# Three ranks of priority for the recurrence stage of a two-block kernel: delta rule, gated branch, conditioning

## The chip, the cores and the metric

One Trainium2 chip, one core. The metric is the time of one execution on the device in microseconds, as the median of several executions. The profile is of one execution, and its times are those of the hardware profiler.

## What is computed

One sequence of 512 latent tokens with 256 context tokens, 1024 channels, everything in float32. `first_block` modulates a LayerNorm, projects it by `w_in` and sends the parts through three branches: a pooling branch, a delta rule and a gated recurrence, each of the last two in both directions. Their outputs, gated, go through `w_out`; a second block (a mixer, two feed-forward parts, latent attention) follows. What the change touches is these two recurrences, cut here to their steps:

```python
def step(S, inp):                       # delta rule, per head, 64 x 64 state
    w_t, k_t, v_t, kk_t, a_t = inp[:5]
    sa = jnp.einsum('bhvk,bhk->bhv', S, kk_t)
    S = (S * w_t[:, :, None, :] - sa[..., None] * (kk_t * a_t)[:, :, None, :]
         + v_t[..., None] * k_t[:, :, None, :])
    y = jnp.einsum('bhvk,bhk->bhv', S, inp[5]) if emit else None
...
def step(S, inp):                       # gated branch, per chunk of 32 tokens
    k_c, i_c, lf_c = inp[:3]
    g = jnp.cumsum(lf_c, axis=2)
    ...
    scores = jnp.einsum('bhtk,bhsk,bhtsk->bhts', q_c, k_c, rel)
    o = inter + jnp.einsum('bhts,bhsv->bhtv', scores, i_c)
    S = (jnp.exp(g_last[:, :, 0, :])[..., None] * S
         + jnp.einsum('bhsk,bhsv->bhkv', k_c * jnp.exp(g_last - g), i_c))
```

Conditioning is a product of the conditioning vectors with large weights (`mod_w`, `ada_w`), which gives shifts and scales; those of `ada_w` are needed only by the second block.

## The kernel before

Activations lie with channels on the partitions and tokens on the free axis. Every dense product (`dense`, L277) works in two float32r parts: the input is split into hh and hl, each weight block of 128 x 512 comes by DMA (`wblock`, L260) and is split by ScalarE (whi, L263) and VectorE (wlo, L264), and TensorE adds hh by whi, hl by whi and hh by wlo.

`block1` has three stages: LayerNorm and modulation into hh, hl; the recurrence stage; and the product with `w_out` with a LayerNorm. The recurrence stage consists of

- the **delta rule** (`rwkv_pair`), three pairs of heads p = 0 to 2 one after the other. A pair makes dense k, v and r, normalises kk (L631), and prepares (`rwkv_prep`): up-products for decay and a (L689), exponentials, and from them the operands BK and AR on VectorE (BK at L727). Then come three groups of four chunks. A group first makes scores of AR and BK (L763) and inverts a triangular matrix; a chunk updates the state (L926, L928, L934, L943), and the groups 1 and 2 give outputs (L959, L960). After each group but the last a gate (`gate`, a dense product and a sigmoid) is made. At the end of a pair is a readout (L658, L662).
- the **gated branch** (`hgrn_pair`), three pairs, each with a dense q, a dense i (transposed at L996), and for each direction a dense z and a unit (`hgrn_unit`), so six units, 0 to 5. A unit makes levels and gates on VectorE and ScalarE, then goes through its chunks: scores (L1084, L1087, L1091) copied by ScalarE into sct (L1099, L1102, L1104), outputs (L1111, L1112), state (L1120, L1125). A pair ends with a norm (L1008).
- **conditioning** (`ada`): half a block of `mod_w` and six blocks of `ada_w`, each block 16 transfers of 512 KB (L315) and the products of 4 columns of blocks with each (L318), then a copy (adaev) and transposes (L324).
- the **pooling branch** and, at the end, `gated`, the products of outputs and gates.

In PSUM, the delta rule has the banks mm, rsc and rch, the gated branch mf, conditioning ma. What follows in time on each engine is decided by the scheduler of the language when the program is built: it takes, of what is ready by its own estimate, the instruction with the lowest priority number, and that number counts up in the order in which the program is written. Before, a loop of six wrote one or two steps of the delta rule, one unit of the gated branch and one block of conditioning per turn, so the three had about the same priority at each point. On the chip each engine takes its instructions in the order so fixed.

Of the kernel before, what the change touches and what calls it, by code (L numbers as in the profile page):

```python
# [197 lines left out]
class B:  # L198
    def __init__(self, ctx, tc, d, taps=()):
        self.tc, self.nc, self.d, self.taps = tc, tc.nc, d, taps  # L200
        self.ctx = ctx
        self.cst = ctx.enter_context(tc.tile_pool(name="cst", bufs=1))
        self.wp = ctx.enter_context(tc.tile_pool(name="wp", bufs=3))
        self.hp = ctx.enter_context(tc.tile_pool(name="hp", bufs=1))
        self.streams = {"m": (self.wp, 2, 2)}
        self.load_consts()

    @contextmanager
    def banks(self, **spec):
# [217 lines left out]
    def block1(self):  # L427
        nc, tc, d = self.nc, self.tc, self.d
        mod = self.cst.tile([128, 24, 2], F32, name="mod")
        sc1 = self.cst.tile([128, 8, 2], F32, name="sc1")  # L430
        self.m2 = [self.cst.tile([128, 48, 2], F32, name=f"m2{l}") for l in range(2)]
        s = self.cond(self.cst)
# [15 lines left out]
        with ExitStack() as ctx:  # L448
            ctx.enter_context(self.banks(mm=2, rsc=2, rch=1, mf=2, ma=1))
            ctx.enter_context(self.stream("f", 2, 1))  # L450
            ctx.enter_context(self.stream("a", 3, 1))
            self.scr = ctx.enter_context(tc.tile_pool(name="scr", bufs=1, space=bass.MemoryType.DRAM))
            self.f1 = ctx.enter_context(tc.tile_pool(name="f1", bufs=1))
            self.f2 = ctx.enter_context(tc.tile_pool(name="f2", bufs=2))
            self.con1 = self.f1.tile([128, CONST.shape[1] - NCON], F32, name="con1")
            nc.sync.dma_start(self.con1, d["const"][:, NCON:])
            self.ymix = self.scr.tile([128, 8, NL], F32, name="ymix")
            self.ygate = self.scr.tile([128, 8, NL], F32, name="ygate")
            self.ar = [[self.f1.tile([128, 4, 2, 2 if g else 1, 64], F32, name=f"AR{g}{dd}") for dd in range(2)] for g in range(3)]
            self.tt = self.f1.tile([128, 8, 2, 64], F32, name="rtt")  # L460
            for a in (*chain(*self.ar), self.tt):
                nc.gpsimd.memset(a, 0.0)
            self.sct = [self.f1.tile([128, 2, 128], F32, name=f"sct{a}") for a in range(2)]
            for x in self.sct:
                nc.gpsimd.memset(x, 0.0)
            self.rwkv_lora()
            self.hgrn_lb()
            self.last = {}
            rw = chain.from_iterable(self.rwkv_pair(p) for p in range(3))
            hg = chain.from_iterable(self.hgrn_pair(p) for p in range(3))  # L470
            next(rw)
            for n in range(6):
                for _ in range(2 - n % 2):
                    next(rw, None)
                next(hg)
                if n == 0:
                    self.ada(s, 0, d["mod_w"], 1, 2, mod[:, 16:24], self.V("mod_b", 16, 8), "a")
                    self.pool_branch()
                l, g = divmod(n, 3)
                self.ada(s, 2, d["ada_w"][l], g, 4, self.m2[l][:, 16 * g:16 * g + 16],  # L480
                         self.V("ada_b_2", 48 * l + 16 * g, 16), "a")
            hh, hl = self.htiles()

            def gated(j, y=None):
                a = y or self.f1.tile([128, NL], F32, tag=("tw", "ta")[j % 2], name="ga")
                b = self.f1.tile([128, NL], F32, tag=("G", "km")[j % 2], name="gb")
                if y is None:
                    nc.sync.dma_start(a, self.ymix[:, j])
                nc.sync.dma_start(b, self.ygate[:, j])
                nc.gpsimd.tensor_tensor(b, a, b, op=ALU.mult)  # L490
                self.split(hh[:, j, 256:], hl[:, j, 256:], b)

            for j in (0, 1, 2, 3, 5, 6):
                gated(j)
            for _ in chain(rw, hg):
                pass
            for j in (4, 7):
                gated(j, self.last[j])
        self.xp = self.ctx.enter_context(tc.tile_pool(name="xp", bufs=1, reuse_waits="tile"))
# [115 lines left out]
    def rwkv_pair(self, p):  # L615
# [25 lines left out]
        for g in range(3):  # L641
            pre = self.rwkv_pre(g, bk, v)
            sts = []
            for i in range(4):
                sts.append(st)
                st = self.rwkv_chunk(g, i, ec[:, :, 4 * g + i], pre, st)
            if g:
                self.rwkv_out(g, sts, pre, y)
            if 3 * p + g < 8:
                self.gate(3 * p + g)  # L650
            if g < 2:
                yield

# [1127 lines left out]
```

## Time and profile before

| | us |
|---|---|
| median of 3 executions | 2722.59 |
| lowest and highest | 2719.27, 2726.03 |
| the profiled execution | 2736.78 |
| its span | 2735.0 |
| TensorE busy in the span | 2523.7 (92%) |
| VectorE, ScalarE busy | 1621.3 (59%), 1276.9 (47%) |
| mean granted clock of TensorE in the span | 0.947 |

A row of the view of waits gives the engine, the line that waited and its output, what it waited for, the total, how often and the longest. A row of the timeline gives start and duration, the instruction and, in brackets, the idle time before it and what ended that. The granted clock is a share of full speed: 1.00 is the upper of two levels, 0.50 the lower. The rows themselves stand in the section ahead of the prediction.

### The profile page before, as it was taken

The numbers are of one execution on the slowest core, as the hardware profiler recorded it, in microseconds if no ns is written. First come the engines' busy times: TensorE is split into PE (matmuls) and PEld (weight loads), VectorE is DVE, ScalarE is ACT, GpSimd is POOL, SyncE is SP. The second block draws the span as 40 slices with busy tenths as digits, with TensorE's granted clock in tenths as the row PEclk, the third lists the DMA queues.
The fourth block names the chain that finished last, engine by engine and source line by source line (L and its number), as shares of the span: only waits on it lengthen the run. The fifth ranks groups of instructions, "written<-read, shape, count | busy, mean of one in ns | idle before, by whom it ended". The sixth has DMA issues, their size and how long they took to land.

```text
span 2735.0 us, 53289 instructions
## 1 busy us (share of the span) xinstructions
PE 2523.7 (92%) x21320; PEld 1990.5 (73%) x21320; DVE 1621.3 (59%) x3815; ACT 1276.9 (47%) x2840; POOL 319.3 (12%) x432
## 2 busy tenths in 40 slices
PE   7989979979877989989899999999998999999998
PEld 3655646545546777777677888888886888888888
DVE  4566574576565656777856443344463767664665
ACT  3454454545455656556434332233344555542444
POOL 0121121122112000111110110011000000010010
PEclk9999989989887999999989999999998999999999
DMA  6233432434334211111231112212231102233325
GB/s 206 77 94 118 139 98 92 125 100 134 93 104 146 72 39 32 36 41 37 65 105 47 62 63 64 63 63 66 80 105 44 32 27 95 78 100 93 100 89 157
DMA packets 159016, 231.10 MB, mean 84 GB/s; under 512 B 12976, under 2 KB 90032, under 8 KB 158768
## 3 DMA queue, kind: packets, MB, share of 16 engines
q1 hardware_dynamic: 158768, 227.70, 26.7%
q8 instruction: 167, 2.74, 0.4%
q14 instruction: 81, 0.66, 0.1%
HBM read 217.95 MB, written 9.70 MB: 83 GB/s over the span
## 4 chain that ended last, share of the span: by engine, by line
PE 47%; DVE 2%; ACT 2%; issue 1%; POOL 1%; DMA 0%; POOLq 0%; SPq 0%; DVEq 0%; ACTq 0%
PE mm L277 39%; PE ms L1735 2%; PE mt L1754 1%; PE mv L351 1%; PE mt L1748 1%; PE mm L1685 1%; PE mf L277 0%; DVE hl L423 0%; DVE ht L421 0%; POOL qr L1669 0%; ACT hh L422 0%; DMA raw<-mla_w_out 0%; ACT whi L263 0%; ACT qrh L1705 0%; PE mm L1665 0%
## 5 line engine op out<-in xcount | busy, mean ns | idle before, releaser
L264 DVE TENSOR_TENSOR wlo<-raw,whi 128x512 fp32r<-128x512 f32 (+3 forms) x560 | 391.3, 701 | 395.1 <-ACT whi L263 236.6
L263 ACT CAST whi<-raw 128x512 fp32r<-128x512 f32 (+3 forms) x560 | 331.9, 594 | 462.8 <-PE mm L277 398.9
L277 PE MATMUL mm<-hh,whi 128*128 128x512 f32 (+1 forms) x1960 | 483.8, 360 | 28.0 <-ACT hh L422 13.6
L277 PE MATMUL mm<-hl,whi 128*128 128x512 f32 (+1 forms) x1960 | 457.3, 350 | 0.0
L277 PE MATMUL mm<-hh,wlo 128*128 128x512 f32 (+1 forms) x1960 | 455.3, 350 | 0.4 <-DVE wlo L264 0.4
L277 PEld LDWEIGHTS mm<-hh,whi 128*128 128x128 f32 x1960 | 332.4, 192 | 89.7 <-ACT hh L422 21.0
L277 PEld LDWEIGHTS mm<-hl,whi 128*128 128x128 f32 x1960 | 329.7, 193 | 46.8 <-issue 3.6
L277 PEld LDWEIGHTS mm<-hh,wlo 128*128 128x128 f32 x1960 | 328.9, 193 | 45.0 <-issue 2.0
L1233 POOL TENSOR_TENSOR fc<-fc,fc 128x768 f32<-128x768 f32 (+1 forms) x44 | 69.2, 1573 | 867.9 <-DVE fc L585 625.8
L277 PE MATMUL mm<-fh,whi 128*128 128x256 f32 (+1 forms) x616 | 136.3, 340 | 1.0 <-ACT fh L398 1.0
L583 DVE SCALAR_TENSOR_TENSOR fc<-mm,vec,fc 128x511 f32<-128x511 f32 (+1 forms) x132 | 86.8, 658 | 80.7 <-ACT fc L582 80.7
L277 PE MATMUL mm<-fl,whi 128*128 128x256 f32 (+1 forms) x616 | 130.5, 330 | 0.0
L277 PE MATMUL mm<-fh,wlo 128*128 128x256 f32 (+1 forms) x616 | 129.3, 328 | 0.0
L582 ACT ACTIVATE fc<-mm,vec 128x512 f32<-128x512 f32 (+1 forms) x132 | 81.4, 617 | 97.2 <-PE mm L277 97.2
L277 PEld LDWEIGHTS mm<-fh,whi 128*128 128x128 f32 x616 | 99.8, 190 | 15.8 <-issue 3.4
L318 PE MATMUL ma<-raw,cvs 128*32 128x256 f32 x832 | 95.6, 427 | 15.3 <-DMA raw<-ada_w 10.6
L277 PE MATMUL mf<-hh,whi 128*128 128x512 f32 (+1 forms) x360 | 103.6, 387 | 6.0 <-ACT whi L263 3.4
L277 PEld LDWEIGHTS mm<-fl,whi 128*128 128x128 f32 x616 | 99.0, 190 | 11.3 <-issue 0.5
L1197 DVE SCALAR_TENSOR_TENSOR xr<-mm,m,xr 128x512 f32<-128x512 f32 (+1 forms) x112 | 66.5, 597 | 67.0 <-PE mm L277 66.8
L277 PEld LDWEIGHTS mm<-fh,wlo 128*128 128x128 f32 x616 | 98.6, 190 | 10.4
L351 PE MATMUL mv<-sq,con 128*128 128x256 f32 (+1 forms) x240 | 84.3, 452 | 12.4 <-ACT sq L355 12.0
L277 PE MATMUL mf<-hl,whi 128*128 128x512 f32 (+1 forms) x360 | 95.4, 367 | 0.0
(545 smaller groups left out, 4383.6 us busy)
## 6 DMA issues: line engine op xcount, KB each, us to landing
raw<-ada_w SPq DMA_DIRECT2D x96, 512.0 KB, 4.6
raw<-ffn_up SPq DMA_DIRECT2D x176, 256.0 KB, 2.8
raw<-ffn_down SPq DMA_DIRECT2D x96, 256.0 KB, 2.7
raw<-w_in SPq DMA_DIRECT2D x66, 256.0 KB, 2.9
raw<-ab_w_in SPq DMA_DIRECT2D x50, 256.0 KB, 2.6
raw<-ffn_down SPq DMA_DIRECT2D x48, 192.0 KB, 2.4
raw<-mod_w SPq DMA_DIRECT2D x16, 512.0 KB, 7.6
raw<-w_out SPq DMA_DIRECT2D x32, 256.0 KB, 2.9
```

The costliest lines, as they stand in the source:

```text
L263: nc.scalar.copy(hi[:, :nk], raw[:, :nk])
L264: nc.vector.tensor_tensor(lo[:, :nk], raw[:, :nk], hi[:, :nk].bitcast(F32), op=ALU.subtract)
L277: nc.tensor.matmul(o, a[:, k], b[:, k0 + k, t:e], start=(k0 == 0 and j == 0 and k == 0), stop=(k0 + n == nk and j == 2 and k == n - 1))
L318: nc.tensor.matmul(acc[32 * b:32 * b + 32, c:c + 256], s[:, k, :], t[:, b], start=(k == 0), stop=(k == 7))
L351: self.nc.tensor.matmul(v[:, :x.shape[1]], self.C("ones"), x, start=(k == 0), stop=(k == 7))
L582: nc.scalar.activation(out[:, c0:c0 + cn], o[:, :cn], AF.Copy, scale=w[1])
L583: nc.vector.scalar_tensor_tensor(out[:, c0 + 1:c0 + cn], o[:, :cn - 1], w[0], out[:, c0 + 1:c0 + cn], op0=ALU.mult, op1=ALU.add)
L1197: nc.vector.scalar_tensor_tensor(x, o[:, :cn], gcol(m, 0 if c0 else 1), x, op0=ALU.mult, op1=ALU.add)
L1233: nc.gpsimd.tensor_tensor(g, g, u, op=ALU.mult)
L1685: nc.tensor.matmul(o[:, e], a[:, k, T], b[:, k], start=(i == 0), stop=(i == 5))
L1735: nc.tensor.matmul(o[:, at:at + cn], a, b, start=(j == 0), stop=(j == 4))
L1748: nc.tensor.transpose(tp[:, j], p[:, (c0 + j) * 128:(c0 + j + 1) * 128], self.C("ident"))
```

## The change

`ranks(3)` takes the current priority number as the base of rank 0 and sets rank 1 100000 above it and rank 2 200000 above it, and one more as the place after all of them. Inside `rank(i)` instructions are numbered on in that rank. The delta rule's steps are written in rank 0, the gated branch's units in rank 1, conditioning in rank 2. `behind(400)` moves the gates and the pooling branch back by 400 numbers in the delta rule's rank. The loop has nine turns instead of six, with a delta-rule step in each, a gated unit in six and a block of conditioning in seven; what is left of both recurrences is written after it, and `gated` after all ranks. No computation is changed, and the number of instructions is the same on every engine.

```diff
--- before.py
+++ after.py
@@ -204,6 +204,25 @@
         self.hp = ctx.enter_context(tc.tile_pool(name="hp", bufs=1))
         self.streams = {"m": (self.wp, 2, 2)}
         self.load_consts()
+
+    def ranks(self, n):
+
+        self.rank_at = [self.tc.cur_priority + 100000 * i for i in range(n + 1)]
+
+    @contextmanager
+    def rank(self, i):
+        tc, now = self.tc, self.tc.cur_priority
+        tc.cur_priority = self.rank_at[i]
+        yield
+        self.rank_at[i] = tc.cur_priority
+        tc.cur_priority = now
+
+    @contextmanager
+    def behind(self, n):
+
+        self.tc.cur_priority += n
+        yield
+        self.tc.cur_priority -= n
 
     @contextmanager
     def banks(self, **spec):
@@ -468,17 +487,32 @@
             self.last = {}
             rw = chain.from_iterable(self.rwkv_pair(p) for p in range(3))
             hg = chain.from_iterable(self.hgrn_pair(p) for p in range(3))
-            next(rw)
-            for n in range(6):
-                for _ in range(2 - n % 2):
+            self.ranks(3)
+            with self.rank(0):
+                next(rw)
+            for n in range(9):
+                with self.rank(0):
                     next(rw, None)
-                next(hg)
-                if n == 0:
-                    self.ada(s, 0, d["mod_w"], 1, 2, mod[:, 16:24], self.V("mod_b", 16, 8), "a")
-                    self.pool_branch()
-                l, g = divmod(n, 3)
-                self.ada(s, 2, d["ada_w"][l], g, 4, self.m2[l][:, 16 * g:16 * g + 16],
-                         self.V("ada_b_2", 48 * l + 16 * g, 16), "a")
+                    if n == 0:
+                        with self.behind(400):
+                            self.pool_branch()
+                if n % 3 != 2:
+                    with self.rank(1):
+                        next(hg)
+                with self.rank(2):
+                    if n == 0:
+                        self.ada(s, 0, d["mod_w"], 1, 2, mod[:, 16:24], self.V("mod_b", 16, 8), "a")
+                    elif n < 7:
+                        l, g = divmod(n - 1, 3)
+                        self.ada(s, 2, d["ada_w"][l], g, 4, self.m2[l][:, 16 * g:16 * g + 16],
+                                 self.V("ada_b_2", 48 * l + 16 * g, 16), "a")
+            with self.rank(0):
+                for _ in rw:
+                    pass
+            with self.rank(1):
+                for _ in hg:
+                    pass
+            tc.cur_priority = self.rank_at[3]
             hh, hl = self.htiles()
 
             def gated(j, y=None):
@@ -492,8 +526,6 @@
 
             for j in (0, 1, 2, 3, 5, 6):
                 gated(j)
-            for _ in chain(rw, hg):
-                pass
             for j in (4, 7):
                 gated(j, self.last[j])
         self.xp = self.ctx.enter_context(tc.tile_pool(name="xp", bufs=1, reuse_waits="tile"))
@@ -647,7 +679,8 @@
             if g:
                 self.rwkv_out(g, sts, pre, y)
             if 3 * p + g < 8:
-                self.gate(3 * p + g)
+                with self.behind(400):
+                    self.gate(3 * p + g)
             if g < 2:
                 yield
 
```

What this does to the order of TensorE is shown at three places. A row is a group of program instructions, and the trace counts two records for most of them. Lines below the new functions are 19 to 33 higher than before.

**First place: the preparation of the delta rule's pair 2.** Before, on TensorE, from the last rows of a gated unit's dense product to the second scores (L763):

```order
L277 MATMUL mf<-hh,whi 128x256 x4
L277 MATMUL mf<-hl,whi 128x256 x4
L277 MATMUL mf<-hh,wlo 128x256 x4
L318 MATMUL ma<-raw,cvs 32x256 x11
L763 MATMUL rsc<-AR_386,BK_6561 128x128 x4
L318 MATMUL ma<-raw,cvs 32x256 x3
L689 MATMUL mm<-xa,aup 128x512
L689 MATMUL mm<-xa,aup 128x256
L318 MATMUL ma<-raw,cvs 32x256 x17
L763 MATMUL rsc<-AR_387,BK_6562 128x128 x3
L734 MATMUL mm<-rpb,con 128x512
L1120 MATMUL mf<-con,hkd 128x128 x2
```

Now, on TensorE, the up-products (L722, L689 before) of pair 2; rch and rsc are PSUM of the delta rule's chunks and outputs of the pair before (L959, L961, L967 and L976 were L926, L928, L934 and L943):

```order
L722 MATMUL mm<-xa,aup 128x256
L959 MATMUL rch<-uv,scs 64x64 x2
L961 MATMUL rch<-rS,AR_390 64x64
L961 MATMUL rch<-rS,AR_391 64x64
L959 MATMUL rch<-uv,scs 64x64 x2
L961 MATMUL rch<-rS,AR_390 64x64
L961 MATMUL rch<-rS,AR_391 64x64
L992 MATMUL rsc<-AR_390,rS 64x64
L722 MATMUL mm<-xw,wup 128x512
L967 MATMUL rch<-xs,rtt 64x64 x4
L722 MATMUL mm<-xw,wup 128x256
L1144 MATMUL mf<-hqe,hS 64x128
```

And the scores of pair 2 (L796, L763 before) with what stands ahead of them:

```order
L691 MATMUL rsc<-ry,con 128x512
L337 MATMUL ma<-raw,cvs 32x256 x8
L695 MATMUL rsc<-rsq,con 128x512
L722 MATMUL mm<-xa,aup 128x512
L722 MATMUL mm<-xa,aup 128x256
L796 MATMUL rsc<-AR_386,BK_7236 128x128 x4
L337 MATMUL ma<-raw,cvs 32x256 x3
L1117 MATMUL mf<-hlv 32x32 x8
L767 MATMUL mm<-rpb,con 128x512
L796 MATMUL rsc<-AR_387,BK_7237 128x128 x4
L813 MATMUL rsc<-con,BK_7236 128x128 x4
```

The up-products stood behind all chunks of the pair before and beside the gated branch's dense product; three quarters of them have moved up between the last chunks of that pair, and the scores follow soon behind that pair's readout (L691, L695).

**Second place: the end of the delta rule.** Before, on TensorE, from the last state update (L943) on; mf is PSUM of the gated branch, ma of conditioning:

```order
L943 MATMUL rch<-uv,bkt 64x64 x4
L960 MATMUL rsc<-scs,uv 64x64
L959 MATMUL rsc<-AR_391,rS 64x64
L960 MATMUL rsc<-scs,uv 64x64
L318 MATMUL ma<-raw,cvs 32x256 x4
L658 MATMUL rsc<-ry,con 128x512
L1120 MATMUL mf<-con,hkd 128x128 x2
L1125 MATMUL mf<-hit,hkt 64x64 x4
L662 MATMUL rsc<-rsq,con 128x512
L1084 MATMUL mf<-hlv 32x32 x36
L1084 MATMUL mf<-hq,hz 32x32 x4
L1084 MATMUL mf<-hlv 32x32 x4
```

Now, from the same update (L976) on:

```order
L976 MATMUL rch<-uv,bkt 64x64 x4
L993 MATMUL rsc<-scs,uv 64x64
L992 MATMUL rsc<-AR_391,rS 64x64
L993 MATMUL rsc<-scs,uv 64x64
L1117 MATMUL mf<-hlv 32x32 x15
L1117 MATMUL mf<-hq,hz 32x32 x4
L1120 MATMUL mf<-hlv 32x32 x2
L1124 MATMUL mf<-hlv 32x64 x2
L1144 MATMUL mf<-hqe,hS 64x128
L1145 MATMUL mf<-sct_400,hit 64x128
L691 MATMUL rsc<-ry,con 128x512
L1144 MATMUL mf<-hqe,hS 64x128
L1153 MATMUL mf<-con,hkd 128x128
```

Before, the last unit's scores stood behind that end; now it is a unit of the pair before (unit 2) that emits there, and three units are still to come.

**Third place: the dense product for z of unit 3.** Before, on TensorE, it stood among pair 2's up-products:

```order
L689 MATMUL mm<-xa,aup 128x256
L277 MATMUL mf<-hh,wlo 128x512
L689 MATMUL mm<-xw,wup 128x512
L689 MATMUL mm<-xw,wup 128x256
L277 MATMUL mf<-hh,whi 128x256 x4
L277 MATMUL mf<-hl,whi 128x256 x4
L277 MATMUL mf<-hh,wlo 128x256 x4
L318 MATMUL ma<-raw,cvs 32x256 x8
L277 MATMUL mf<-hh,whi 128x512 x4
L277 MATMUL mf<-hl,whi 128x512 x4
L277 MATMUL mf<-hh,wlo 128x512 x4
```

Now, with unit 2's last outputs (L1144, L1145) ahead of it:

```order
L1144 MATMUL mf<-hqe,hS 64x128
L337 MATMUL ma<-raw,cvs 32x256 x4
L1145 MATMUL mf<-sct_400,hit 64x128
L1144 MATMUL mf<-hqe,hS 64x128
L296 MATMUL mf<-hh,whi 128x512 x3
L1145 MATMUL mf<-sct_400,hit 64x128
L296 MATMUL mf<-hh,whi 128x512
L296 MATMUL mf<-hl,whi 128x512 x4
L296 MATMUL mf<-hh,wlo 128x512 x4
L296 MATMUL mf<-hh,whi 128x256 x4
L296 MATMUL mf<-hl,whi 128x256 x4
L296 MATMUL mf<-hh,wlo 128x256 x4
```

It has moved from the preparation of the delta rule's pair 2 to a place behind the delta rule's end.

## Rows read from the trace of the kernel before

**Rows 1.** The page: busy times by engine, and the clock in 40 slices.

```profile
PE 2523.7 (92%) x21320; PEld 1990.5 (73%) x21320; DVE 1621.3 (59%) x3815; ACT 1276.9 (47%) x2840; POOL 319.3 (12%) x432
...
PEclk9999989989887999999989999999998999999999
```

**Rows 2.** Stretches: length, busy PE, PEld, DVE, ACT, POOL; clock, DMA share, GB/s.

```profile
81.00:849.00 768.00, 661.35 (x9773) 427.80 (x9771) 468.78 (x1331) 382.82 (x1150) 147.77 (x265) 0.88 0.34 107
...
340.00:380.00 40.00, 26.18 (x288) 13.95 (x286) 34.68 (x77) 20.85 (x56) 12.91 (x22) 0.68 0.38 120
...
580.00:620.00 40.00, 25.12 (x240) 13.86 (x230) 36.78 (x79) 18.90 (x50) 12.64 (x16) 0.70 0.44 138
...
800.00:849.00 49.00, 25.39 (x515) 14.15 (x513) 29.86 (x84) 25.02 (x101) 13.73 (x18) 0.55 0.35 114
...
81.00:654.00 573.00, 506.20 (x7049) 329.02 (x7048) 363.80 (x1011) 286.50 (x818) 115.14 (x211) 0.90 0.35 108
...
654.00:849.00 195.00, 155.16 (x2725) 98.78 (x2724) 104.98 (x320) 96.32 (x333) 32.64 (x54) 0.83 0.33 103
```

**Rows 3.** Timeline of TensorE, preparation of the delta rule's pair 2.

```profile
563.35 1.02 PE L631 MATMUL mm<-kksq,con 128*128 128x512 f32 x2
...
584.43 2.05 PE L763 MATMUL rsc<-AR,BK 128*128 128x128 f32 x8 [3.30 <-DVE BK L727]
...
604.69 1.62 PE L763 MATMUL rsc<-AR,BK 128*128 128x128 f32 x6 [7.69 <-DVE BK L727]
```

**Rows 4.** Waits of TensorE, 81 to 654 us.

```profile
PE rsc L763 <- DVE BK L727: 18.3, 4, 7.7
...
PE ma L318 <- DMA raw<-ada_w: 8.2, 9, 2.8
...
PE ma L324 <- DVE adaev L321: 4.2, 1, 4.2
...
PE ma L318 <- DMA raw<-mod_w: 2.9, 3, 1.4
```

**Rows 5.** Timeline of TensorE, gated units 4 and 5 and the delta rule's end.

```profile
697.13 0.79 PE L277 MATMUL mf<-hh,whi 128*128 128x512 f32 x1
...
719.25 0.63 PE L277 MATMUL mf<-hh,wlo 128*128 128x256 f32 x3
...
741.45 0.48 PE L1111 MATMUL mf<-hqe,hS 128*64 128x128 f32 x1
...
765.74 0.80 PE L277 MATMUL mf<-hh,whi 128*128 128x512 f32 x1
...
766.46 0.69 PE L1112 MATMUL mf<-sct,hit 128*64 128x128 f32 x2
...
785.73 0.74 PE L277 MATMUL mf<-hh,wlo 128*128 128x256 f32 x4
...
797.42 0.45 PE L943 MATMUL rch<-uv,bkt 128*64 128x64 f32 x8 [0.28 <-ACT uv L939]
...
812.29 0.45 PE L1111 MATMUL mf<-hqe,hS 128*64 128x128 f32 x1 [1.14 <-ACT sct L1104]
...
839.26 0.69 PE L1112 MATMUL mf<-sct,hit 128*64 128x128 f32 x2 [0.90 <-ACT sct L1099]
...
849.06 1.22 PE L351 MATMUL mv<-sq,con 128*128 128x256 f32 x2 [5.54 <-ACT sq L355]
```

**Rows 6.** Lines of TensorE, 81 to 849 us: conditioning, the gated branch's dense products.

```profile
L318 PE MATMUL ma<-raw,cvs 128*32 128x256 f32 x832 | 95.6, 427 | 15.3 <-DMA raw<-ada_w 10.6 <-DMA raw<-mod_w 2.9 <-ACT sct L1099 1.6
...
L277 PE MATMUL mf<-hh,whi 128*128 128x512 f32 (+1 forms) x168 | 49.5, 392 | 0.5 <-ACT whi L263 0.5
...
L277 PE MATMUL mf<-hl,whi 128*128 128x512 f32 (+1 forms) x168 | 46.0, 372 | 0.0
...
L277 PE MATMUL mf<-hh,wlo 128*128 128x512 f32 (+1 forms) x168 | 46.5, 376 | 0.0
```

## The prediction

> **What bounds the kernel now.** I read the page first: TensorE is busy for 2523.7 of 2735.0 us, far ahead of the other engines, and its granted clock is full in most slices [rows 1]. Time can therefore come from two places only: TensorE's idle time, and stretches at the lower clock. Then I cut the table of stretches to the part that the change can move. The two orders are the same up to the first gate (about 150 us) and again from the middle of the last gated unit, so the recurrence stage, 81 to 849 us, is the whole field: 768 us, 661.35 busy, 106.65 idle, clock 0.88 [rows 2]. The instructions themselves are the same in number and kind; nothing is removed or added, so the whole effect is order.
>
> The losses inside the stage are not even. Two stretches, 340:380 and 580:620, hold 26.18 and 25.12 us of TensorE work in 40 us at clocks 0.68 and 0.70, while VectorE has 34.68 and 36.78 [rows 2]: these are the preparations of pairs 1 and 2 of the delta rule. The chain of VectorE work from the normalisation of kk (L631) to the scores (L763) is long: in pair 2 it runs from 563.35 to 604.69, some 41 us, and TensorE stands still for 3.30 and 7.69 us at its end [rows 3]. Its four waits are the stage's largest, 18.3 us [rows 4]. The third weak stretch is the end, 800:849: 25.39 us of work in 49, clock 0.55 [rows 2]. There the last gated unit runs alone, since the delta rule's last state update is at 797.42 [rows 5].
>
> **The change part by part.** TensorE takes its instructions in the written order, so each effect is a wait filled or a wait laid bare.
>
> *Cut of the stage.* With ranks, the delta rule's last chunk comes ahead of unit 3's dense product for z (the third place shown from the order), and what remains then is units 3, 4 and 5 of the gated branch, the change of pair between 3 and 4, and three conditioning blocks. How much TensorE work is that? Conditioning: six and a half blocks hold 832 records and 95.6 us, a block 128, so three take 3 x 128 x 95.6 / 832 = 44 us [rows 6]. Dense products of the gated branch: 49.5 + 46.5 + 46.0 = 142 us for three pairs [rows 6], of which a pair's z, z, q and i take 1.5, 1.5, 1 and 1.5 parts in 5.5 (12.9 us for a z). Three z and one q and i are 38.7 + 21.5 = 60 us. Emission: the stretch 800:849 is nearly one unit's and holds 25.39 us at a low clock [rows 2]; without the delta rule's readout and the norms (about 6 us) it is 19, or 17 at the stage's mean clock; three make 51. Sum 155 us. By the same amount of work the kernel before divides at 654 us: 506.20 us of work in 573 us up to there, then 155.16 in 195 [rows 2].
>
> *First part (573 us now, idle 573 - 506.20 = 66.8).* The two preparation stretches have 80 - 26.18 - 25.12 = 28.7 us idle. In the new order the next pair's up-products stand between the last four chunks of the pair before (the first place shown from the order), so VectorE's chain runs beside chunks, outputs and gated scores rather than beside conditioning alone. The four chunks and the group's outputs last about 18 us of the 41; I take half of the idle off: 14 remain (bounds: 6, if all is covered, as pair 0's cost is not touched; and 28.7, if nothing is). The waits for conditioning are 8.2 for its weights, 4.2 for its evicted tile and 2.9 for the modulation weights, 15.3 us [rows 4]. Conditioning is last in rank now and three of its blocks leave this part: 8 remain (bounds 5 and 15.3). The other 22.8 us are short waits within chunks and units; I leave 20 (15 to 22.8). So 42 us idle (26 to 67). The clock: at 0.68 and 0.70, 64% and 60% of these stretches were granted the lower of the two levels (1.2 against 2.4 GHz), which is 16.8 and 15.1 us of their work; at the full clock that work takes half, 16 us less. With half of the holes filled I take half, 8 (0 to 16). First part: 506.2 - 8 + 42 = 540 us, a gain of 33.
>
> *Tail (195 us now).* A unit is a serial chain: dense z, gates and levels on VectorE and ScalarE, scores, outputs, with ScalarE's sct copies before each output. From unit 4: the z product ends at 719.9 and the first output starts at 741.45, 22 us; the outputs last to 767.1, 26 us. Unit 5: 786.4 to 812.3, 26, and to 839.9, 28 [rows 5]. The z product itself takes 20 to 23 us beside the delta rule [rows 5], and 12.9 of work alone. A lone unit is then 12 + 22 + 26 = 60 us (bounds: 55, from a faster VectorE and ScalarE when the delta rule is gone; and before's own period, 697.13 to 765.74 = 68.6). Units 3 and 4 are 120. The change of pair is 21.5 of q and i products, and the transposes and the norm: 28 (25 to 28). Unit 5 to the stage's end is 12 + (849.06 - 786.4 = 62.7) = 75, less 4 for the delta rule's last chunks that lay beside it: 71 (68 to 83). Tail: 219 us (203 to 248). It is 24 us longer than before's last 195, for it holds 160 us of work (155 and some 5 to 7 at the low clock) with 59 idle.
>
> *The rest.* The gates and the pooling branch move 400 places back, behind the delta rule's next group; all still stand ahead of unit 3, among work of the first part, and their dense products are filler: 0. If that cover went, they would stand in the tail, whose holes of 59 us would hide them as well. SP issues the conditioning's transfers; 48 of 512 KB, 25.2 MB, move behind the delta rule. Over 219 us this is 115 GB/s, and the stage as a whole moved 107 with 138 in 580:620 [rows 2], so the transfers fit; where a weight of the gated branch is queued behind one that waits for a free buffer, the wait is at most the 2.8 us that a starved conditioning matmul waited [rows 4]: 0 taken, 10 at worst. POOL, with 12% [rows 1], bears no part of it. The gating products that are written later keep their place: 0.
>
> *Sum.* 540 + 219 = 759 against 768 us: -9. The profiled execution took 2736.8 us (span 2735.0), 14.2 above the median of the runs, 2722.6. So 2736.8 - 9 = 2728 on its basis, **2714 us** on the median's.
>
> **The rule that speaks against it.** In the stretch where all three parts mix, TensorE is full; in 800:849, where the gated branch is alone, it works 52% of the time at clock 0.55 [rows 2]. The Trainium skill, Perfetto Trace Analysis, Optimization Strategy, says that a kernel whose busiest engine changes between regimes may gain from interleaving the regimes. The change takes a part of such interleaving away, and by that rule the result would be the first rival below. The row agrees with the rule as to the end of the stage, but the two preparation stretches are holes inside the mixture that it does not heal.
>
> **The rivals.**
> 1. *The lone tail costs more than the filled holes: slower.* Units 3 to 5 run alone at before's period and end: 2 x 68.6 + 28 + 83 = 248 us, where the first part stays 540: 788, +20, or **2743 us**. For it: the clock of 0.55 and the waits for sct in 800:849. Against it: before's period holds delta-rule work that will be gone, and three blocks of conditioning fill the holes. It decides once the tail passes 228 us, a unit of about 64.
> 2. *The two cancel.* The chain of a preparation is VectorE's own length, so its end is no earlier against the chunks that it is mixed with, and 28.7 us of holes shrink by only a third: first part 545 to 550, tail 219: **2722 us**.
> 3. *Much is gained.* If the first part comes near the waits of the well-filled rest (idle 26, clock full: 506 - 16 + 26 = 516) and the tail is 228, the sum is 744, -24: **2699 us**.
> 4. *The change does nothing.* The order shows otherwise: the delta rule's end moves ahead of half the gated branch. I give it no chance.
>
> **How the numbers follow.** Forecast 0.40, rival 1 0.28, rival 2 0.16, rival 3 0.16. A measurement here can tell about 0.3%, 8 us, from no change. The forecast lies near that line: of its 0.40, 0.26 are faster, 0.12 the same and 0.02 slower. With rival 3 faster has 0.42, with rival 2 the same 0.28, slower 0.30. The forecast's own range, first part 530 to 550 and tail 210 to 228, is 2695 to 2733. For 8 in 10 I reach over rival 1 with its worst transfer waits and just past rival 3: 2692 to 2748.
>
> **What would show it.** Right: the delta rule ends near 620 us, not 797; the waits L763 for BK fall from 18.3 to under 10; no 40-us stretch ahead of 600 is below 30 us of work; TensorE works some 160 of the last 219 us of the stage, and units 3 to 5 are about 60 us apart. Wrong: units over 64 us apart with the clock near 0.55 for the whole tail (rival 1); waits for BK as large as before, at other places (rival 2); or long waits of the gated branch's weights behind conditioning's.

## The result, and the profile after

The change is slower: 2757.7 us against 2724.3, medians of four runs each, a ratio of 1.0113 (95% interval 1.0078 to 1.0147). A second series of the same kernel gave 1.0095 (1.0080 to 1.0111), 26 us. The forecast was 2714, its range 2692 to 2748: wrong in sign and outside the range.

The page of the kernel after, busy times and clock [rows 1]:

```profile
PE 2527.8 (92%) x21320; PEld 1997.8 (72%) x21320; DVE 1617.8 (59%) x3815; ACT 1275.2 (46%) x2840; POOL 318.2 (12%) x432
...
PEclk8998899897886999999989999999999999999999
```

In the profiled executions the span grew by 22 us, 2735.0 to 2756.9, less than the medians' 33: before's profiled execution, 2736.8 us, lay 12 us above its median, the change's 1 us. The stage now ends at 872.07 us instead of 849.06: it has all of the loss, and the rest of the program is one us shorter. The stretches, from the table of stretches (columns as in [rows 2]): the stage, the first part up to unit 3's product for z, the tail, and the preparations of pairs 1 and 2:

```profile
81.00:872.00 791.00, 662.47 (x9761) 432.22 (x9759) 466.30 (x1328) 380.56 (x1148) 146.80 (x263) 0.86 0.33 104
...
81.00:674.00 593.00, 512.89 (x7632) 347.04 (x7630) 372.52 (x1058) 286.62 (x796) 121.11 (x223) 0.90 0.27 85
...
674.00:872.00 198.00, 149.58 (x2133) 85.19 (x2129) 93.78 (x270) 93.94 (x353) 25.68 (x40) 0.74 0.51 162
...
300.00:345.00 45.00, 35.58 (x345) 19.89 (x344) 35.87 (x75) 24.23 (x58) 11.27 (x28) 0.81 0.43 140
...
470.00:513.00 43.00, 26.44 (x290) 14.15 (x289) 39.96 (x95) 22.37 (x58) 19.51 (x35) 0.84 0.24 73
```

The work is the same as before, 662.47 us against 661.35, at nearly the same clock, 0.86 against 0.88. The idle time is 128.5 us against 106.65: that is the loss. The first part takes 593 us, 80.1 of them idle, where 540 and 42 were forecast; the tail 198, where 219 was forecast. The two preparations have 9.4 + 16.6 = 26.0 us of idle against 28.7 before, though TensorE was to have work beside them. What TensorE waited for in the first part (the view of waits, 81 to 674 us):

```profile
PE mm L767 <- POOL rpb L765: 10.3, 2, 9.3
PE mf L1117 <- DVE hlv L1072: 7.9, 3, 4.9
PE ma L337 <- DMA raw<-ada_w: 6.7, 7, 1.6
PE mf L1144 <- ACT sct L1137: 6.3, 3, 3.2
PE rsc L894 <- DVE rsh L879: 5.9, 6, 2.6
PE rsc L894 <- issue: 5.9, 4, 1.8
PE mm L604 <- POOL rx L875: 4.6, 1, 4.6
PE rsc L796 <- DVE BK L760: 3.8, 2, 2.2
PE rsc L841 <- DVE rw L838: 3.8, 4, 2.0
PE ma L337 <- DMA raw<-mod_w: 3.4, 3, 1.5
...
PE ma L343 <- DVE adaev L340: 1.7, 3, 1.0
```

Before, BK made it wait 18.3 us at the scores [rows 4]. Now L796 waits 3.8 us for BK, but the order has put L767, the sum for the bonus term, ahead of those scores, and L767 waits 10.3 for the same chain of VectorE, through POOL. The timeline of TensorE in pair 2's preparation, from kk (L663) to the second scores:

```profile
466.09 1.12 PE L663 MATMUL mm<-kksq,con 128*128 128x512 f32 x2
...
492.40 1.55 PE L722 MATMUL mm<-xa,aup 64*128 64x512 f32 x4
493.88 1.16 PE L796 MATMUL rsc<-AR,BK 128*128 128x128 f32 x8
494.97 0.63 PE L337 MATMUL ma<-raw,cvs 128*32 128x256 f32 x6
500.46 0.36 PE L1117 MATMUL mf<-hlv 64*32 64x32 f32 x16 [4.86 <-DVE hlv L1072]
510.15 2.08 PE L767 MATMUL mm<-rpb,con 128*128 128x512 f32 x2 [9.33 <-POOL rpb L765]
512.02 1.57 PE L796 MATMUL rsc<-AR,BK 128*128 128x128 f32 x8
```

Between 494.97 and 512.02 TensorE has six conditioning records and sixteen gated scores to do. VectorE works all that time, for the most part on the second direction's AR (L747), BK (L757, L758, L760) and bonus term (L764). From its timeline:

```profile
493.56 1.14 DVE L723 TENSOR_SCALAR ta<-mm,vec 128x512 f32<-128x512 f32 x2 [1.11 <-PE mm L722]
...
501.19 4.31 DVE L747 TENSOR_TENSOR AR<-tw,rkk 64x252 f32<-64x252 f32 x6
505.53 1.05 DVE L757 TENSOR_TENSOR BK<-km,G 128x768 f32<-128x768 f32 x1
506.50 0.95 DVE L758 TENSOR_TENSOR ta<-ta,rkk 128x768 f32<-128x768 f32 x1
507.37 0.74 DVE L764 SCALAR_TENSOR_TENSOR km<-km,vec,rr 128x512 f32<-128x512 f32 x1
508.03 0.94 DVE L760 TENSOR_TENSOR BK<-ta,G 128x768 f32<-128x768 f32 x1
```

The hole has moved and changed its name; it has hardly shrunk. And new waits stand in the list: of the triangular inverse (L894) 5.9 us for VectorE and 5.9 for nothing that the profile shows, of the pooling branch's product (L604) 4.6, of gated scores for VectorE's levels (L1117) 7.9.

The tail, from the timeline of TensorE (delta rule's last state update; z of unit 3, its first and last outputs; z of unit 5, its last output; the stage's end), against [rows 5]:

```profile
651.31 0.45 PE L976 MATMUL rch<-uv,bkt 128*64 128x64 f32 x8
...
674.15 1.65 PE L296 MATMUL mf<-hh,whi 128*128 128x512 f32 x3
...
705.85 0.43 PE L1144 MATMUL mf<-hqe,hS 128*64 128x128 f32 x2
...
731.97 0.43 PE L1145 MATMUL mf<-sct,hit 128*64 128x128 f32 x2
...
805.89 0.96 PE L296 MATMUL mf<-hh,whi 128*128 128x512 f32 x3
...
862.39 0.69 PE L1145 MATMUL mf<-sct,hit 128*64 128x128 f32 x2 [0.90 <-ACT sct L1132]
...
872.07 1.22 PE L370 MATMUL mv<-sq,con 128*128 128x256 f32 x2 [5.41 <-ACT sq L374]
```

Unit 3 takes 674.15 to 732.4, 58 us, where 60 was forecast; unit 4 with the change of pair takes 73, to 805.89, where 88 was forecast; unit 5 to the end 66, where 71 was forecast.

### The profile page after: what moved, and what is told of

Same layout as the page of the kernel before. It is cut to its first block, busy times and chain, and to the rows that moved or that the text cites. A ratio compares the mean times of both kernels' runs of the same rounds, so it can differ in the third digit from the quotient of the medians.

```text
span 2756.9 us, 53313 instructions
## 1 busy us (share of the span) xinstructions
PE 2527.8 (92%) x21320; PEld 1997.8 (72%) x21320; DVE 1617.8 (59%) x3815; ACT 1275.2 (46%) x2840; POOL 318.2 (12%) x432
## 4 chain that ended last, share of the span: by engine, by line
PE 46%; DVE 2%; ACT 2%; POOL 1%; issue 1%; DMA 0%; POOLq 0%; DVEq 0%; ACTq 0%
PE mm L296 39%; PE ms L1768 2%; PE mv L370 1%; PE mt L1787 1%; PE mt L1781 1%; PE mm L1718 1%; PE mf L296 0%; DVE hl L442 0%; DVE ht L440 0%; ACT whi L282 0%; POOL qr L1702 0%; DMA raw<-mla_w_out 0%; POOL qr L1701 0%; ACT hh L441 0%; ACT qrh L1738 0%
## 5 line engine op out<-in xcount | busy, mean ns | idle before, releaser
L337 PE MATMUL ma<-raw,cvs 128*32 128x256 f32 x832 | 109.0, 466 | 29.7 <-DMA raw<-ada_w 25.7
L296 PEld LDWEIGHTS mm<-fh,whi 128*128 128x128 f32 x616 | 99.9, 190 | 15.7 <-issue 3.4
```

The lines of the kernel that those rows point to most:

```text
L296: nc.tensor.matmul(o, a[:, k], b[:, k0 + k, t:e], start=(k0 == 0 and j == 0 and k == 0), stop=(k0 + n == nk and j == 2 and k == n - 1))
L337: nc.tensor.matmul(acc[32 * b:32 * b + 32, c:c + 256], s[:, k, :], t[:, b], start=(k == 0), stop=(k == 7))
```

## The experiments

Ratios are to before, run beside each variant, with the 95% interval; before's median moved between 2724 and 2731 us from series to series, so the differences, not the times, are to be compared. One per mille is 2.7 us. One caution stands over all of them: with every edit the scheduler decides the whole order anew, so a difference of some 10 us between two variants need not come from the edit's own place.

**Taking the change apart.** Four kernels: the ranks without the moves back, the moves back without the ranks, conditioning alone in a last rank, and delta rule first with one rank for the others.

```diff
-                        with self.behind(400):
+                        with self.behind(0):
...
-                with self.behind(400):
+                with self.behind(0):
```

> The three ranks stay, the gates and the pooling branch are not moved back (0 in place of 400). Theory A (the split of delta rule and gated branch leaves the last three gated units alone and the delta rule's own holes unfilled): within 8 us of the change, 2750 to 2766. Theory B (the gates, moved behind the next group, leave the start of each group bare, where TensorE waited for the triangular inverse for 13 us): 15 us or more faster than the change, 2730 to 2742, and the waits of L894 fall to under 5 us.

Measured: 1.0041 (1.0026 to 1.0055), 11 us slower than before. Theory A asked for the change's own loss, theory B for some 10 us over before; B comes nearer, and all waits of L894 together fell from 12.8 to 7.5 us, not under 5. So the ranks alone cost 11 us, and the moves back cost 15 to 20 more within them (1.0095 or 1.0113, from the change's two series). Without the moves the hole of the preparations keeps its old name, and the ranks have not healed it either (view of waits, 81 to 640 us):

```profile
PE rsc L796 <- DVE BK L760: 13.0, 3, 9.8
```

```diff
                 if n == 0:
...
-                    self.pool_branch()
+                    with self.behind(400):
+                        self.pool_branch()
...
             if 3 * p + g < 8:
-                self.gate(3 * p + g)
+                with self.behind(400):
+                    self.gate(3 * p + g)
```

> The order of before, with only the gates and the pooling branch moved back by 400. Theory A: within 8 us of before, 2716 to 2732. Theory B: 15 us or more slower than before, 2740 to 2755.

Measured: 0.9889 (0.9873 to 0.9904), 30 us faster. Both theories missed: the same move that costs inside the ranks gains in the old order.

```diff
-                    self.ada(s, 0, d["mod_w"], 1, 2, mod[:, 16:24], self.V("mod_b", 16, 8), "a")
+                    with self.rank(1):
+                        self.ada(s, 0, d["mod_w"], 1, 2, mod[:, 16:24], self.V("mod_b", 16, 8), "a")
...
-                self.ada(s, 2, d["ada_w"][l], g, 4, self.m2[l][:, 16 * g:16 * g + 16],
-                         self.V("ada_b_2", 48 * l + 16 * g, 16), "a")
+                with self.rank(1):
+                    self.ada(s, 2, d["ada_w"][l], g, 4, self.m2[l][:, 16 * g:16 * g + 16],
+                             self.V("ada_b_2", 48 * l + 16 * g, 16), "a")
```

> The order of before, with conditioning alone in a rank behind everything. Theory A: within 8 us of before or somewhat faster, 2712 to 2732. Theory C (conditioning in the last rank is what costs: its copy and transposes at a block's end come last on VectorE, so that its one PSUM bank stays taken and it cannot fill the preparations): slower by 12 us or more, 2736 or above, with the idle of the two preparations above the 28.7 us of before.

Measured: 1.0015 (1.0003 to 1.0027), 4 us slower. Theory C falls: the preparations' idle is 22 us, less than before's. The gated branch's last output came at 819 us instead of 840, but then conditioning ran alone to the stage's end:

```profile
821.00:857.00 36.00, 19.56 (x149) 10.22 (x147) 5.75 (x14) 4.95 (x9) 5.81 (x6) 0.68 0.84 275
```

36 us, with its transfers at 275 GB/s. What the recurrences won, the rest of conditioning took back.

```diff
-                with self.rank(2):
+                with self.rank(1):
```

> Delta rule first, gated branch and conditioning together in the second rank, in the order in which they are written. Theory A: still slow, 2745 to 2762, the delta rule's last state update still near 650 us. Theory C: at least half of the loss comes back, 2728 to 2741.

Measured: 1.0130 (1.0115 to 1.0146). Conditioning's own rank was not the loss. As far as the delta rule's place goes (last update at 644 us) it is as theory A said; at 2769 us it is slower still than its bound.

**Is it the separation?** If so, taking the gated branch back into the delta rule's rank, with all else as in the change, must win the loss back:

```diff
-                    with self.rank(1):
+                    with self.rank(0):
                         next(hg)
...
-            with self.rank(1):
+            with self.rank(0):
                 for _ in hg:
                     pass
```

> The change with the gated branch taken back into the delta rule's rank, in the order in which the loop writes them; conditioning stays last, gates and pooling branch stay 400 back. Theory A (the separation of the two recurrences is what costs): faster than before by 8 us or more, 39 us or more against the change. If it stays slower than before by 8 us or more, the separation is not what costs, and theory A falls.

Measured: 0.9951 (0.9930 to 0.9972), 13 us faster than before and some 40 faster than the change: theory A's bounds are met. But in this kernel the moves of 400, too, count in one numbering for both recurrences, as in the order of before, where they gain by themselves. Without any move the separation is worth far less: the ranks alone took 2744.0 us and conditioning alone in the last rank, with both recurrences in the old order, 2735.8, measured side by side. So some 8 of the 40 us are the separation's own, and the rest comes only with the moves. The recurrences ended at 802 us; the last 46 us are lone conditioning, as in the third kernel above:

```profile
802.00:848.00 46.00, 24.46 (x183) 11.43 (x181) 6.46 (x15) 4.89 (x9) 5.72 (x6) 0.65 0.83 266
```

And the opposite separation, gated branch first:

```diff
-            with self.rank(0):
+            with self.rank(1):
                 next(rw)
...
-                    with self.rank(1):
+                    with self.rank(0):
                         next(hg)
...
```

> The three ranks with the first two exchanged: gated branch first, delta rule second, conditioning last, gates as in the change. Differences are to before in the same call. Theory A (any full separation ends in a lone chain whose holes nothing fills): 8 to 50 us slower than before, the last gated output ahead of 600 us and a lone delta-rule end of 150 us or more with over 30 us idle. Theory F (only the gated branch is bad to be alone, for its outputs wait for ScalarE's copies; the delta rule alone has the gates and its own dense products to fill): no slower than before, within 8 us or faster.

Measured: 1.0234 (1.0204 to 1.0263), 64 us slower than before, more than theory A asked, and the slowest of all. The last gated output came at 602 us and a lone delta rule was left. The stretch lasts 306 us, 81.6 of them idle:

```profile
605.00:911.00 306.00, 224.43 (x3591) 148.47 (x3589) 145.90 (x419) 106.61 (x260) 63.09 (x101) 0.79 0.31 100
```

Its largest wait, in the view of waits, is that of the inverse for VectorE:

```profile
PE rsc L894 <- DVE rt L887: 17.8, 6, 9.8
```

So it is not only the gated branch that is bad to be alone; the delta rule is too. (Here, too, the moves of 400 are in place; gated branch first without them was not run.)

**What bounds the first part?** A preparation with less VectorE work, first in the change, then in before. Both kernels leave out the products for a part of AR, so they do not compute all of the delta rule:

```diff
-                        nc.vector.tensor_tensor(ar[H, :, h, 0, 1:64], e[H, cs, 0:63], kkv[H, cs, 1:64], op=ALU.mult)
...
-                        nc.vector.tensor_tensor(ar[H, :, h, 0, 0:63], e[H, cs, 1:64], kkv[H, cs, 0:63], op=ALU.mult)
```

> The change, without the 36 VectorE products that multiply kk by the decay into AR (they take about 4 us in each direction of each pair); that part of AR stays zero, so this part of the delta rule is left out. Theory P (VectorE's chain sets the length of a preparation, so the order of TensorE cannot fill it): each direction of pairs 1 and 2 gets shorter by 3 to 4 us, the kernel by 12 to 24 us against the change, that is from 10 us faster to 20 us slower than before. Theory A alone (the loss is in the tail): under 8 us faster than the change.

> Before, without the 36 VectorE products that multiply kk by the decay into AR (that part of the delta rule is left out, as in the short preparation of the change, which was 30 us faster than the change). Theory P (VectorE's chain sets a preparation's length in either order): 20 to 35 us faster than before. If the ranks did hide the preparation better than before does, the change would gain less by it than before: over 40 us faster here.

Measured: in the change 1.0005 (0.9991 to 1.0018), 24 to 29 us faster than the change's two series, a little over what theory P asked, with 14.3 us of idle in the two preparations (the rows below) in place of 26.0; in before 1.0007 (0.9989 to 1.0025), no gain. Of the two alternatives for before neither came.

```profile
287.00:330.00 43.00, 35.41 (x374) 19.92 (x372) 33.50 (x76) 26.18 (x63) 18.55 (x32) 0.92 0.39 125
...
440.00:480.00 40.00, 33.26 (x538) 18.28 (x536) 33.40 (x87) 27.50 (x72) 15.58 (x33) 0.97 0.48 150
```

These stretches end ahead of the second scores. From kk to the second scores the preparations of pairs 0, 1 and 2 took 32, 34 and 45 us, in the change 41, 44 and 46, and those of pairs 1 and 2 hold 15.7 us of idle in place of 27.2. So the chain got shorter in two of the three pairs; in the third other VectorE work filled the place of what was left out.

In before the shorter chain did take the waits for BK away, but other waits, those for conditioning's weights first of all, grew in their place (10.6 us before [rows 6]; view of waits, 81 to 845 us):

```profile
PE ma L318 <- DMA raw<-ada_w: 19.2, 17, 2.6
...
PE rsc L761 <- DVE BK L725: 3.0, 1, 3.0
```

The idle time of its stage is 104 us, where before has 107. As far as these two kernels show it, the chain of the delta rule sets the time only where it is ranked first. The stretches of four profiles, up to the end of the delta rule's readout and from there to the stage's end (the change; the ranks alone; the short preparation; the change's second profile):

```profile
81.00:658.00 577.00, 501.55 (x7383) 340.68 (x7381) 362.82 (x1029) 277.45 (x754) 120.46 (x221) 0.91 0.27 85
...
658.00:872.00 214.00, 160.92 (x2379) 91.54 (x2378) 103.48 (x301) 103.10 (x394) 26.34 (x42) 0.73 0.49 156
```

```profile
81.00:640.00 559.00, 489.12 (x7402) 333.76 (x7401) 362.28 (x1029) 277.32 (x755) 122.00 (x221) 0.94 0.29 89
...
640.00:854.40 214.40, 159.85 (x2354) 91.07 (x2354) 102.86 (x299) 102.87 (x394) 26.35 (x42) 0.73 0.48 153
```

```profile
81.00:625.00 544.00, 486.31 (x7376) 332.14 (x7375) 345.29 (x989) 277.17 (x754) 126.36 (x220) 0.95 0.28 89
...
625.00:838.30 213.30, 157.94 (x2380) 90.42 (x2378) 104.27 (x302) 103.16 (x394) 24.60 (x44) 0.75 0.49 157
```

```profile
81.00:650.00 569.00, 492.47 (x7377) 335.27 (x7375) 361.60 (x1025) 277.22 (x754) 120.39 (x221) 0.93 0.28 86
...
650.00:864.00 214.00, 159.81 (x2380) 90.85 (x2379) 103.77 (x302) 103.37 (x394) 26.91 (x43) 0.73 0.50 157
```

The second stretch is 213 to 214 us in all of them, with 158 to 161 us of work at a clock of 0.73 to 0.75: units 3 to 5 and conditioning, whatever came ahead. All differences stand in the first stretch, 544 to 577. Not all of them are the order's: the change's two profiles are of one and the same kernel and differ by 8 us, with 75.5 and 76.5 us idle and clocks of 0.91 and 0.93. In idle time, the ranks alone have 69.9 and the short preparation 57.7. Under the ranks the stage is thus a sum: the delta rule's chain, and a lone tail. The tail is not a constant: it was 233 us where conditioning shared the gated branch's rank, and 197 where the moves were 200 (further below), with 147 us of work in it, since unit 2 was further on by then.

**The moves back.** The pooling branch put back, in the change and in the moves alone:

```diff
-                        with self.behind(400):
-                            self.pool_branch()
+                        self.pool_branch()
```

> The change with the pooling branch in its old place; the ranks stay and the gates stay 400 back. Differences are to before in the same call, where the change itself is 31 us slower and the ranks with neither moved 11 us slower. Theory G (inside the ranks too the pooling branch is the harmful one of the two moves, the gates are neutral or good): no more than 11 us slower than before. Theory D (in the ranks 400 numbers are a whole group, and the gates are what harms): 20 us or more slower.

> The order of before with the gates alone moved back by 400, the pooling branch in its old place. If the gates are what made the kernel with both moved back 30 us faster than before: 20 to 35 us faster than before here too. If the pooling branch is: within 8 us of before.

Measured: in the change 1.0061 (1.0043 to 1.0079), 17 us slower than before, between what the two theories asked; in the order of before 0.9843 (0.9811 to 0.9875), **44 us faster than before**, the fastest of all and more than the 20 to 35 asked. The pooling branch's move costs 9 to 14 us in either order (1.0113 or 1.0095 against 1.0061; 0.9889 against 0.9843); what the gates' move costs inside the ranks, 1.0041 to 1.0061, is within the intervals. The pooling branch takes its tiles from the same buffers as the preparation (the tags tw, G and km in the kernel); whether that is why its move costs, no run tells. The fastest kernel's stage:

```profile
81.00:795.00 714.00, 631.13 (x9760) 412.74 (x9759) 466.73 (x1327) 378.81 (x1148) 142.82 (x265) 0.93 0.36 115
```

54 us shorter than before [rows 2]: 83 us idle in place of 107, and 30 us less busy for the same instructions, at a clock of 0.93 in place of 0.88. By the medians it is 44: before's profiled execution lies 12 us above its median, this one 4 below.

The distance of the moves, in the change (200 for 400), and in the order of before (800 with the pooling branch, 800 and 200 for the gates alone), each by its number alone, here the first:

```diff
-                        with self.behind(400):
+                        with self.behind(200):
                             self.pool_branch()
...
-                with self.behind(400):
+                with self.behind(200):
                     self.gate(3 * p + g)
```

> The change with 200 in place of 400 for both moves, half a group of the delta rule in its own numbering. Theory D: faster than the ranks with neither moved, under 11 us slower than before, since the gates now fill the next group's start. Theory G: between the ranks with neither moved and the change, 12 to 31 us slower, since the pooling branch is still moved.

> The order of before with the gates and the pooling branch moved back by 800 numbers in place of 400. In before all three parts count in one numbering, and a group of the delta rule comes every 896 numbers on average, so 400 is under half of that and 800 nearly a whole; in the ranks the delta rule counts alone, a group every 407 to 649, and 400 is a whole one. Theory D (the gates gain when they move by about half a group and lose when they pass a whole one): slower than with 400 by 10 us or more, 0 to 20 us faster than before. Theory E (the later the gates, the better, for their dense products fill the end): as fast as with 400 or faster, 25 us or more faster than before.

> The order of before with the gates alone moved back, by 800 in place of 400 (with 400: 44 us faster than before). Theory E (the later the better): 44 us faster or more. Theory D (about half a group is best): 10 us or more behind the 400.

> The order of before with the gates alone moved back by 200 (400: 44 us faster than before, 800: 29). Theory D (an optimum near half a group): between the two ends, 10 to 40 us faster than before. If the gain comes from anything else than the gates' distance, it is the same 44 again, or none.

Measured: 1.0067 (1.0048 to 1.0087); 0.9901 (0.9880 to 0.9923); 0.9891 (0.9856 to 0.9927); 0.9975 (0.9963 to 0.9988). For the gates alone 200, 400 and 800 give 7, 44 and 29 us: an optimum in between, as theory D has it, though the 7 lie below its 10 to 40. But with the pooling branch moved too, 800 lost nothing against 400 (27 and 30 us): there theory E's number came, against theory D. Inside the ranks 200 numbers fell on theory G's side. Why 400 is so good is not settled.

> The change itself, beside its variants on one chip: 25 to 36 us slower than before.

Measured: 1.0095 (1.0080 to 1.0111), 26 us, as expected.

And the gated branch in the delta rule's rank, with the pooling branch put back:

```diff
-                        with self.behind(400):
-                            self.pool_branch()
+                        self.pool_branch()
                 if n % 3 != 2:
-                    with self.rank(1):
+                    with self.rank(0):
                         next(hg)
...
```

> The change with both recurrences in one rank and the pooling branch in its old place; conditioning stays last, the gates 400 back. If the parts add up (one rank for both gave 44 us against the change, the pooling branch back 15): 22 to 34 us faster than before. If conditioning in the last rank bounds it (its lone end is 36 us in the order of before with conditioning last): no better than with the pooling branch moved, 8 to 18 us faster than before.

Measured: 0.9951 (0.9936 to 0.9966), 13 us faster, the same as without the pooling branch's return, so here its move costs nothing. That is the number of the second alternative, and conditioning does end alone (37 us, from 792 to 829.5); that this lone end takes what else is won is not shown.

## Why the prediction was wrong

*The cut held, and the tail was not the loss.* The stage did become a first part and a lone tail, though the delta rule ended at 651 us and not near 620. The tail, 219 forecast, was 198, below the bounds of 203 to 248; a lone unit, 60 forecast, was 58, and unit 4 with the change of pair, 88 forecast, was 73; the tail's work, 160 forecast, was 150. The first rival had the sign right, but its price, a tail of 248, was not paid.

*The steps that failed are "First part", 540 us, which took 593, and the 0 for the moves back, whose cost fell into it.* The terms one by one:

- "I take half of the idle off: 14 remain" of the preparations' holes: 26.0. The row that would have said so was there: in these stretches VectorE was busy for 34.68 and 36.78 of 40 us [rows 2], and the chain itself lasted 41 us [rows 3]. Up-products that come earlier on TensorE do not help where VectorE sets the pace; from kk at 466 us to the second scores at 512 it now took 46 us. The second rival had this mechanism, but priced its idle alone; its sign, waits as large at other places, came: 3.8 for BK and 10.3 at L767, where BK's were 18.3.
- "The other 22.8 us are short waits ...; I leave 20": 80.1 - 26.0 and less 11.8 for conditioning is 42.3. The inverse (12.8), the units' levels (L1117, 7.9) and the pooling branch (4.6) stood bare; that three of six units had gone to the tail and that the units' VectorE work came last is the likely reason, not a tested one. Nothing in the trace of before priced these waits, and the bound of 22.8 rested on the belief that what is ranked first gets its fill from what is ranked last. It was also too low by itself: the two preparation stretches of before already hold 5.5 us of the waits for conditioning's weights (2.8 and 2.7), which the sum takes off twice.
- "The gates and the pooling branch move 400 places back ...: 0": with both moves undone the loss was 11 us in place of 26 to 31, so they cost 15 to 20 us, more than half of it; the pooling branch's move alone 9 to 14. With them the inverse waited 12.8 us in place of 7.5 and the pooling branch's product 4.6. That the moved products are filler was taken without a row; it was the old order in which the gates' move gained.
- "8 remain" of the waits for conditioning: 6.7 + 3.4 and 1.7 for its copy, 11.8.
- "With half of the holes filled I take half, 8" of the clock: the clock of the first part is 0.90, as before; nothing was won.

The first part misses by 15 us in work and 38 in idle time; of the 15, some 10 are work that the prediction had put into the tail. In the profile the stage as a whole misses by 32 us, 791 against 759. Another 13 us of the median's miss come from the step to the median: 14.2 us were taken off, the distance of before's profiled execution from its median, and the change's own lay 1 us above.

*What stood behind it.* I took the stage as bound by TensorE, so that any order that fills holes gains. Under the ranks it is bound by the first chain and then by the lone rest: shortening the delta rule's chain gained 24 to 29 us there and nothing in before. By steps, conditioning in the last rank cost 4 us, the separation of the recurrences some 8 more, the moves inside the ranks 15 to 20; the first two are no larger than what any new order may make. The Trainium skill's rule on interleaving regimes (Perfetto Trace Analysis, Optimization Strategy) was weighed and set below the filled holes; the runs side with it in sign: one rank for both recurrences is 13 us faster than before, two are 11 to 31 us slower, and the gated branch first 64 us slower. How much of this is the separation and how much the moves that go with it was said above.

*Not settled.* Why the gates 400 numbers back gain 44 us in the old order, why the pooling branch's move costs, and how much of each variant is the scheduler's luck.

## What to carry to other kernels

Before ranking one chain first, ask which engine sets that chain's length: if it is not the one whose holes are to be filled, the holes move with the chain. In this kernel strict ranks turned work that ran side by side into a sum of a first chain and a lone remainder, and the length of a lone unit could be read off the end of the old profile, where the last unit already runs alone. Moving only the independent filler, here the gates' dense products by 400 places, gained more than any ranking; but the same kind of move cost time inside the ranks, so a move that rides along with a change is to be measured by itself and not put at 0.

## What was not expected of the hardware

The clock moved as much time as the waits. Between the profiles of before and of the fastest kernel the idle time differs by 24 us and TensorE's busy time by 30, for the same instructions: 661.35 us at a mean granted clock of 0.88 and 631.13 at 0.93. Not all of the 30 need be the order's: between the two profiles of the change the busy time of the first stretch differs by 9 us (501.55 and 492.47) at the same idle time. In the lone tails the clock was 0.73 to 0.75, and in before's last unit, alone, 0.50:

```profile
805.00:849.00 44.00, 22.90 (x501) 13.13 (x494) 25.29 (x74) 22.11 (x90) 9.64 (x13) 0.50 0.36 115
```
